# A two-layer encoder step: lead-in on two tiles, products added up in PSUM, and token sums begun a tile sooner

## The chip, the cores and the metric

One core of a Trainium2 chip runs the whole program; the other cores are idle. The metric is the device time of one execution in microseconds, the median of several runs. The engines are named as the profile names them: PE (TensorE), DVE (VectorE), ACT (ScalarE), POOL (GpSimd), SP (the queue that issues most DMAs).

## What is computed

Two layers run over 640 rows (512 of a prompt, 8 x 16 of decode streams) of 1024 features. Every layer is

```
h = rmsnorm(x, g0)
a_x, a_b, a_c, dq, dk, dv, fq, fk, fv, ff, pu = split(h @ w_in)
o = (short_conv, differential_attention, forgetting_attention, pooling)
merged = sum_i sigmoid(h @ w_gate[i] + b_gate[i]) * (o[i] @ w_branch[i])
x = x + rmsnorm(merged @ w_out, g1)
h2 = rmsnorm(x, g2); gu = h2 @ w_ffn_in
x = x + rmsnorm((silu(gu[:, :F]) * gu[:, F:]) @ w_ffn_out, g3)
```

with F = 2816. The keys and values of the new rows are outputs too.

## The kernel before

Activations lie transposed in SBUF: 1024 features as eight blocks of 128 partitions, 640 rows as columns. Every matrix is split into a high and a low half (fp32r), and every product is made as high x high + high x low + low x high. ACT copies the high half of a weight (`whi`, `copy`), DVE subtracts it from the raw one to get the low half (`wlo`, line 274); `w_split` queues these two beforehand, `flush` sends the pending subtractions to DVE.

The order of the instructions on each engine is the order in which the program is written: generators for attention, gates and products are driven in turn by a planner (`drive`), which hands out work by a count of units, and timers (`after`, `tick`) place side work at a number of units. Each engine works through its queue in order, so an instruction whose inputs are not there holds up all behind it on that engine. `s` are tiles from 33 slots (`alloc`, `free`; `NSLOT`) that are handed out in turn; PSUM has the banks S (2), D (2 pairs), O and T (1 each).

**Start** (`first`, lines 1933 to 1955): x comes in five tiles of 128 rows, two halves each. For each tile `norm1` squares the rows on ACT (line 344), takes the root on POOL (338) and scales by root and norm weight on DVE (353); `norm2` transposes on PE (361) into S banks and splits into Ph (ACT) and Pl (DVE, 120). The norm weights come by one DMA per half that spreads a row over 128 partitions. `ab_start` makes the first two input products: the first `CUT` = 384 columns (tiles 0 to 2) of both, then the rest, with the work on the last tiles as hooks among the matmuls. The same `ab_start` with the same `CUT` starts each later pair after a mix (`mix_phase`, `start`): three more times. There tile 3 is turned after 2 of the 8 steps of the first product and tile 4 after 6 of the 8 of the second.

**Gates** (`gates`, `strassen_gates`): the third gate phase is made by a seven-product scheme on halves of the matrix (weights `gs`). It needs sums of the rows' halves, `token_sums`: for each of two parts ten adds of 128x640 on DVE (line 483), then splits into high and low. Timers place them from feature block `GATE_F` = 3 on, one per 0.8 x `GATE_STEP` units, while the last decode units of the attention still run. Four slots per part are taken at the first add. The weights' block sums, `weight_sums`, run on POOL (451). `product` (1532) makes 12 matmuls of 320 columns into one bank.

**Feed-forward** (`strassen`, from line 1841): the same seven products for 19 of 22 column blocks per layer. In both, the products are added up by DVE (`add`, 1844 and 1538) in the tiles s1, u2, u3, c22; product 4 is added to product 0 in s1 and goes to ACT's Silu (1863) or tanh (1541), products 3 and 6 are both added to u2.

Of the kernel before, what the change touches and what calls it, by code (L numbers as in the profile page):

```python
# [23 lines left out]
DFF = 2816  # L24
NJ = DFF // 128
HT = T // 2
CUT = 384
NEG = -1e30
BIG = 3.0e38
NSLOT = 33  # L30
ORDER = [0, 1, 2, 3, "v", 4, 5, 6, 7, 12, 13, 9, 10, 14, 11, 15, 8]
P0N = 7
PACE = [2.2] * 16 + [1.8] * 16 + [1.8] + [3.6] * 8 + [5.05] * 9
# [2 lines left out]
FTS = 0.938  # L36
FT0 = 0.0
J0 = 3
GATE_F = 3
GATE_STEP = 0.8  # L40
FO_ORDER = (4, 0, 1, 2, 3, 5, 6, 7, 8, 9, 10)
EPS = 1e-6

# [17 lines left out]
def encoder_step(ctx: ExitStack, tc: tile.TileContext, I, O):  # L61
# [42 lines left out]
    def psS():  # L104
        return pss.tile([128, 512], F32, tag="S", name=nm("S"))
# [248 lines left out]
            xn.append(s)  # L354
        return xn

    def norm2(xn, hi, lo, t):
        for h in range(2):
            ps = psS()
            for c in range(4):  # L360
                PE.transpose(ps[:, c * 128:(c + 1) * 128], xn[h][:, c * 128:(c + 1) * 128], ident)
            pv = ps.rearrange("p (c n) -> p c n", c=4)
            split(hi[:, 4 * h:4 * h + 4, t * 128:(t + 1) * 128], lo[:, 4 * h:4 * h + 4, t * 128:(t + 1) * 128], pv)
            free(xn[h])
# [24 lines left out]
            if k < 7:  # L389
                yield 0.5  # L390

    def ab_start(keys, x, hooks, evac_fn):
        w = []
        Ds = [psD(), psD()]
        for i in range(2):
            w.append([w_sub(keys[i], p, 0) for p in range(2)])
            if i == 0:
                w_split(sidx[keys[1], 1])
                flush()
            dense(Ds[i], w[i], x, (0,), hooks[i])  # L400
        for i in range(2):
            dense(Ds[i], w[i], x, (1,))
            evac_fn(i, Ds[i])
            if i == 0:
                w_ahead(keys[1], 1)
                flush()

    def v2(t):
        return t.rearrange("p (a b) -> p a b", a=2)
# [3 lines left out]
    def big(tag):  # L413
        return hpool.tile([128, 8, T], F32R, tag=tag, name=nm(tag))

    x_first = [load_x(I["x"], t) for t in range(2)]
    g_first = load_g(0, 0)
    ident = const("ident", C_ID, 128)
    mhalf = cpool.tile([128, 8], F32, tag="mhalf", name="mhalf")
    G.memset(mhalf, -0.5)  # L420
    one1 = cpool.tile([128, 1], F32, tag="one1", name="one1")
# [41 lines left out]
    def token_sums(h, dst, at, step=0.6):  # L463
        hv = [f32(x) for x in h]

        def quad(x, r, c, q):
            return hv[x][:, 4 * r + 2 * q:4 * r + 2 * q + 2, c * HT:(c + 1) * HT]

        t = {}
        P_, M_ = ALU.add, ALU.subtract  # L470
        steps = [(0, (0, 1), (0, 0, 0), M_), (0, None, (1, 0, 1), P_), (0, None, (1, 0, 0), M_),
                 (1, (1, 1), 0, M_), (1, None, (1, 1, 1), P_),
                 (3, 1, (0, 1, 0), M_), (3, None, (1, 1, 0), M_),
                 (2, (1, 1), (0, 0, 1), M_), (2, None, (1, 1, 1), P_), (2, None, (1, 0, 1), M_)]

        def form(n, q):
            if n == 0:
                t[q] = [alloc() for _ in range(4)]
            i, a, b, op = steps[n]
            o = v2(t[q][i])  # L480
            a = o if a is None else v2(t[q][a]) if isinstance(a, int) else quad(0, *a, q)
            b = v2(t[q][b]) if isinstance(b, int) else quad(*b, q)
            V.tensor_tensor(out=o, in0=a, in1=b, op=op)
            if n == len(steps) - 1:
                t["formed"] = q

# [509 lines left out]
    def layer(l, Htag, Otag, hT, first_units):  # L996
# [489 lines left out]
        def prepare_gates(f):  # L1486
            if f == 2:
                load_gates(0)
            elif f == GATE_F:
# [12 lines left out]
                gq["t"] = token_sums(hT, dst, 1.0, GATE_STEP)  # L1502
            elif f == 7:
                gate_sums(0)
                need(lambda: gq["t"].get("formed") == 1)
                for k in range(4):
                    src = v2(gq["t"][k // 2][3])[:, k % 2]
                    split(hi[:, k, HT:], lo[:, k, HT:], src)
                free(*[gq["t"][q][3] for q in range(2)])

        def strassen_gates(br, branch):
# [9 lines left out]

            post = []

            def product(ps, n, p):
                wh, wl = w_sub(("gs", l, n), p)
                while post:
                    post.pop(0)()
                xh, xl = moving[p]
                for k in range(4):
                    a, b = wh[:, k * 128:(k + 1) * 128], wl[:, k * 128:(k + 1) * 128]  # L1530
                    for pi, (w, x) in enumerate(((a, xh), (a, xl), (b, xh))):
                        PE.matmul(ps[:, :HT], w, x[k], start=(k == 0 and pi == 0), stop=(k == 3 and pi == 2))  # L1532
                    if k == 1:
                        yield
                out["p"] = ps[:, :HT]
# [12 lines left out]
            for n in range(4):  # L1548
                f = 2 * n
                ta, tb, X, Y = alloc(), alloc(), alloc(), alloc()  # L1550
                s1, u2, u3, c22 = X[:, :HT], X[:, HT:], Y[:, :HT], Y[:, HT:]
                yield from product(psO(), n, 0)
                copy(s1, out["p"])
                yield
                if pend:
# [8 lines left out]
                if pend:  # L1564
                    branch(f - 1, [pend[1]])
                    yield
                yield from product(psT(), n, 3)
                add(c22, out["p"], u3)
                add(u2, out["p"], u2)
                tanh(tb, 1, c22, f + 1)  # L1570
                gate_sums(n + 1)
                yield
                yield from product(psD()[:, 0, :], n, 4)
                add(s1, out["p"], s1)
                tanh(ta, 0, s1, f)
# [5 lines left out]
                yield from product(psS(), n, 6)  # L1581
# [244 lines left out]
        def product(ps, j, p):  # L1826
            wh, wl = w_sub(("fs", l, j), p)
            xh, xl = moving[p]
            for k in range(4):
                a, b = wh[:, k * 128:(k + 1) * 128], wl[:, k * 128:(k + 1) * 128]  # L1830
                for pi, (w, x) in enumerate(((a, xh), (a, xl), (b, xh))):
                    PE.matmul(ps[:, :HT], w, x[k], start=(k == 0 and pi == 0), stop=(k == 3 and pi == 2))  # L1832
                if k == 1:
                    flush()
                    tick(1.0)
            return ps[:, :HT]

        def strassen(j):
# [4 lines left out]
            def add(out, a, b, op=ALU.add):  # L1843
                V.tensor_tensor(out=out, in0=a, in1=b, op=op)  # L1844

            p1 = product(psO(), j, 0)
            for fn in tail[:1]:
                fn()
            copy(s1, p1)
# [5 lines left out]
            p7 = product(psS(), j, 2)  # L1855
            add(u3, p7, u2)
            sums(j + 1)
            p5 = product(psT(), j, 3)
            add(c22, p5, u3)
            add(u2, p5, u2)  # L1860
            p2 = product(psD()[:, 0, :], j, 4)
            add(s1, p2, s1)
            A.activation(out=act[:, :HT], in_=s1, func=AF.Silu)  # L1863
            p4 = product(psD()[:, 0, :], j, 5)
            if j == NJ - 1:
                convert(0)
            add(s1, u3, p4, ALU.subtract)
            add(act[:, :HT], act[:, :HT], s1, ALU.mult)
            p3 = product(psS(), j, 6)
            add(u2, p3, u2)  # L1870

            def gate():
# [57 lines left out]
    with tc.manual_schedule():  # L1930
        h0 = (big("Ph"), big("Pl"))

        def first(evac_fn):
            xn = {}
            turned = lambda t: norm2(xn.pop(t), h0[0], h0[1], t)
            def normed(t):
                xn[t] = norm1(x_first[t], g_first)
                free(*x_first[t])

            normed(0)  # L1940
            normed(1)
            turned(0)
            normed(2)
            turned(1)
            w_split(1)
            flush(G)
            turned(2)
            normed(3)

            def mid():  # L1950
                normed(4)
                turned(3)

            ab_start([("in", 0, c) for c in ORDER[:2]], h0, ({4: mid}, {6: lambda: turned(4)}), evac_fn)
            free(*g_first)

        layer(0, "P", "Q", h0, first)
# [152 lines left out]
```

## Time and profile before

| | us |
|---|---|
| median of 3 runs | 2091.82 |
| lowest and highest | 2089.9, 2094.06 |
| profiled execution | 2095.22 |
| its span, first instruction to last | 2093.4 |
| PE busy in it | 2038.4 (97%) |
| DVE busy | 1491.2 (71%) |
| ACT busy | 981.7 (47%) |
| POOL busy | 429.6 (21%) |

The granted clock of PE is full in nearly every slice of the page. A busy share says little about a single stretch, so the views that matter are PE's waits (who it waited for, how long in total, how often) and the timeline of each engine around them. In a timeline row the first number is the start, the second the time until the last of the merged instructions ended, and the bracket the idle time of the engine before it with what ended that.

### The profile page before, as it was taken

What the parts mean: (1) busy time and instruction counts of PE and PEld (TensorE: products, weight loads), DVE (VectorE), ACT (ScalarE), POOL (GpSimd) and SP (SyncE); (2) the same over time, 40 slices, a digit from 0 to 9 for tenths busy, and PEclk for the clock granted to TensorE, in tenths of its full rate; (3) what the DMA queues carried; (4) which work ended last, traced back from release to release, by engine and by line L of the source; (5) the groups of instructions that cost most, each with busy time, mean ns of one, the idle gap of its engine ahead of it and who ended that gap; (6) DMA issues with size and microseconds to landing.
All of it is one profiled execution on the core that took longest, in us unless ns stands there. A gap on an engine that the chain in (4) does not pass through costs nothing. (4 is left out here: it accounts for less than half of the span.)

```text
span 2093.4 us, 34625 instructions
## 1 busy us (share of the span) xinstructions
PE 2038.4 (97%) x13050; PEld 1928.6 (92%) x13050; DVE 1491.2 (71%) x2914; ACT 981.7 (47%) x2100; POOL 429.6 (21%) x450
## 2 busy tenths in 40 slices
PE   7999999998999999999999999999999999999998
PEld 7999999998989999988889999999988899999887
DVE  5687478698769889853375774876986698888432
ACT  5656355554444344343256553555544443444431
POOL 3211000113013444400040100001130234443000
PEclk9999999999999999999999999999999999999999
DMA  4312244342341222222523122444313422221223
GB/s 148 109 62 79 81 146 140 119 134 73 102 168 62 91 88 84 81 81 71 171 82 110 68 77 82 151 151 141 111 46 130 153 71 90 88 82 61 101 91 121
DMA packets 100743, 214.35 MB, mean 102 GB/s; under 512 B 10896, under 2 KB 35056, under 8 KB 100576
## 3 DMA queue, kind: packets, MB, share of 16 engines
q1 hardware_dynamic: 99552, 209.16, 29.9%
q0 software_dynamic: 1024, 2.98, 0.4%
q8 instruction: 102, 1.67, 0.3%
q14 instruction: 65, 0.53, 0.1%
HBM read 196.02 MB, written 16.08 MB: 101 GB/s over the span
## 5 line engine op out<-in xcount | busy, mean ns | idle before, releaser
L274 DVE TENSOR_TENSOR wlo<-raw,whi 128x512 fp32r<-128x512 f32 (+2 forms) x388 | 267.5, 694 | 160.0 <-ACT whi L117 155.5
L117 ACT ACTIVATE whi<-raw 128x512 fp32r<-128x512 f32 (+2 forms) x390 | 230.5, 606 | 168.6 <-issue 70.6
L274 DVE TENSOR_TENSOR wlo<-s,whi 128x512 fp32r<-128x512 f32 x196 | 205.3, 1048 | 17.5 <-ACT whi L117 16.1
L117 ACT ACTIVATE s<-s 128x512 fp32r<-128x512 f32 (+7 forms) x294 | 175.0, 619 | 77.6 <-DVE s L1420 45.6
L376 PE MATMUL D<-Ph,whi 128*128 128x320 f32 (+2 forms) x736 | 176.9, 315 | 0.9 <-DVE s L1412 0.9
L376 PE MATMUL D<-Qh,whi 128*128 128x320 f32 (+2 forms) x736 | 176.0, 313 | 0.9 <-DVE s L1412 0.9
L376 PE MATMUL D<-Pl,whi 128*128 128x320 f32 (+2 forms) x736 | 173.6, 310 | 0.0
L376 PE MATMUL D<-Ph,wlo 128*128 128x320 f32 (+2 forms) x736 | 173.6, 310 | 0.0
L376 PE MATMUL D<-Qh,wlo 128*128 128x320 f32 (+2 forms) x736 | 172.8, 309 | 0.0
L376 PE MATMUL D<-Ql,whi 128*128 128x320 f32 (+2 forms) x736 | 172.8, 309 | 0.0
L117 ACT ACTIVATE whi<-s 128x512 fp32r<-128x512 f32 x196 | 117.2, 621 | 42.2 <-PE S L1832 18.9
L338 POOL TENSOR_TENSOR r<-ms,mhalf 128x1 f32<-128x1 f32 x40 | 22.0, 551 | 542.1 <-DVE ms L1672 470.4
L376 PEld LDWEIGHTS D<-Ph,whi 128*128 128x128 f32 x736 | 123.0, 189 | 3.6 <-DVE s L1412 1.4
L376 PEld LDWEIGHTS D<-Pl,whi 128*128 128x128 f32 x736 | 125.2, 189 | 0.6 <-DVE Pl L120 0.4
L376 PEld LDWEIGHTS D<-Qh,whi 128*128 128x128 f32 x736 | 122.5, 188 | 3.4 <-DVE s L1412 1.5
L376 PEld LDWEIGHTS D<-Ql,whi 128*128 128x128 f32 x736 | 124.7, 188 | 0.2
L376 PEld LDWEIGHTS D<-Ph,wlo 128*128 128x128 f32 x736 | 124.8, 189 | 0.0
L376 PEld LDWEIGHTS D<-Qh,wlo 128*128 128x128 f32 x736 | 124.3, 188 | 0.0
L744 POOL CAST s<-s 128x16 fp32r<-128x16 f32 x128 | 30.8, 264 | 407.5 <-DVE s L1420 98.2
L451 POOL TENSOR_TENSOR s<-V,V 128x512 f32<-128x512 f32 x48 | 76.1, 1584 | 172.5 <-DMA V<-in_w_fi 85.3
L117 ACT ACTIVATE s<-T 128x320 fp32r<-128x320 f32 (+6 forms) x132 | 50.9, 386 | 106.5 <-PE T L515 62.5
L1863 ACT ACTIVATE s<-s 128x320 f32<-128x320 f32 x38 | 17.9, 472 | 148.4 <-DVE s L1844 148.4
(480 smaller groups left out, 5890.5 us busy)
## 6 DMA issues: line engine op xcount, KB each, us to landing
raw<-in_w_gate SPq DMA_DIRECT2D x48, 512.0 KB, 3.6
raw<-in_w_fi SPq DMA_DIRECT2D x48, 512.0 KB, 3.5
raw<-in_w_fo SPq DMA_DIRECT2D x44, 512.0 KB, 3.5
V<-in_w_fi SPq DMA_DIRECT2D x80, 256.0 KB, 3.0
raw<-in_w_in SPq DMA_DIRECT2D x32, 512.0 KB, 3.3
s<-in_ck_d SPq DMA_DIRECT2D x32, 256.0 KB, 4.1
s<-in_cv_d SPq DMA_DIRECT2D x32, 256.0 KB, 4.1
s<-in_ck_f SPq DMA_DIRECT2D x32, 256.0 KB, 4.1
```

The lines of the kernel that those rows point to most:

```text
L117: A.activation(out=out, in_=in_, func=AF.Copy, scale=scale)
L274: E.tensor_tensor(out=lo, in0=raw, in1=hi, op=ALU.subtract)
L338: G.tensor_tensor(out=out, in0=ssum, in1=mhalf[:, :n], op=ALU.pow)
L376: PE.matmul(Dt[:, h, :c1 - c0], a, b[:, k, c0:c1], start=(start and pi == 0), stop=(stop and pi == 2))
L451: G.tensor_tensor(out=o[:, :512], in0=x, in1=y, op=op)
L744: G.tensor_copy(out=dst[:, 512:KEYS], in_=f32(src[:, 16 * b:16 * b + 16]))
L1863: A.activation(out=act[:, :HT], in_=s1, func=AF.Silu)
```

## The change

`first` loads each norm-weight row once, as 1 x 512, on ACT's DMA queue, and two matmuls with a row of ones spread them over the partitions in a D bank (`gp`). The first two tiles read them there, and ACT copies them to SBUF for the others. `CUT` becomes 256, everywhere: the first part of the first pair covers tiles 0 and 1; in `first` tile 2 is turned after three of eight steps, tiles 3 and 4 later, and some transposes use banks T and O. The early weight split goes to DVE instead of POOL. In both seven-product schemes product 4 is accumulated onto product 0 in bank O, and product 6 onto product 3 in bank T; the two adds fall away. `token_sums` begin at block 2 with a step of 1.0, take each slot at its first use, and there are 36 slots, for which the scratch of POOL's DMAs is halved.

```diff
-CUT = 384
+CUT = 256
-NSLOT = 33
+NSLOT = 36
-GATE_F = 3
-GATE_STEP = 0.8
+GATE_F = 2
+GATE_STEP = 1.0
...
-    x_first = [load_x(I["x"], t) for t in range(2)]
-    g_first = load_g(0, 0)
+    g_first = [alloc(), alloc()]
+    for h in range(2):
+        A.dma_start(out=g_first[h][:1, :512], in_=gbc[0, 0:1, h * 512:(h + 1) * 512])
+    ones = cpool.tile([1, 128], F32, tag="ones", name="ones")
+    G.memset(ones, 1.0)
+    x_first = [load_x(I["x"], 0)]
     ident = const("ident", C_ID, 128)
+    x_first.append(load_x(I["x"], 1))
+    gp = psD()
+    for h in range(2):
+        PE.matmul(gp[:, h, :], ones, g_first[h][:1, :512], start=True, stop=True)
...
-            if n == 0:
-                t[q] = [alloc() for _ in range(4)]
             i, a, b, op = steps[n]
+            if a is not None:
+                t.setdefault(q, {})[i] = alloc()
...
-            p1 = product(psO(), j, 0)
+            pa, pb = psO(), psT()
+            p1 = product(pa, j, 0)
...
-            p5 = product(psT(), j, 3)
+            p5 = product(pb, j, 3)
             add(c22, p5, u3)
-            add(u2, p5, u2)
-            p2 = product(psD()[:, 0, :], j, 4)
-            add(s1, p2, s1)
-            A.activation(out=act[:, :HT], in_=s1, func=AF.Silu)
+            p2 = product(pa, j, 4, True)
+            A.activation(out=act[:, :HT], in_=p2, func=AF.Silu)
...
-            p3 = product(psS(), j, 6)
+            p3 = product(pb, j, 6, True)
             add(u2, p3, u2)
...
             normed(0)
             normed(1)
+            for h in range(2):
+                copy(g_first[h][:, :512], gp[:, h, :])
             turned(0)
+            w_split(0)
+            flush()
+            turned(1, (psT, psO))
             normed(2)
-            turned(1)
-            w_split(1)
-            flush(G)
-            turned(2)
             normed(3)
...
-    nc = bacc.Bacc("TRN2", target_bir_lowering=False, num_devices=1)
+    nc = bacc.Bacc("TRN2", target_bir_lowering=False, num_devices=1, dynamic_dma_scratch_size=8192)
```

The gates' `strassen_gates` is changed in the same way as `strassen`. In the new file lines from 428 on stand 8 to 11 further down (483 is 493, 1420 is 1430, 1844 is 1853).

Where DVE's queue changes, first while the decode units of the forgetting attention run and the second gate phase is at feature block 3, layer 0. Before, from the split of a branch weight on (`rz`, `z`, `m` and `nm` belong to the softmax of a decode unit):

```order
L274 TENSOR_TENSOR wlo_5440<-raw_5275,whi_5439 128x256
L946 RECIPROCAL rz_5353<-z_5352 64x1
L771 MEMSET s_5458 64x128
L775 TENSOR_SCALAR s_5458<-s_5354,rz_5353 64x512
L775 TENSOR_SCALAR s_5458<-s_5354,rz_5353 64x16
L274 TENSOR_TENSOR wlo_5479<-raw_5399,whi_5478 128x512
L933 ISA s_5534,m_5530<-S_5518,s_5534 64x264
```

And now, from the same split on:

```order
L274 TENSOR_TENSOR wlo_5447<-raw_5282,whi_5446 128x256
L493 TENSOR_TENSOR s_5464<-Ph_139 128x640
L956 RECIPROCAL rz_5360<-z_5359 64x1
L781 MEMSET s_5467 64x128
L785 TENSOR_SCALAR s_5467<-s_5361,rz_5360 64x512
L785 TENSOR_SCALAR s_5467<-s_5361,rz_5360 64x16
L493 TENSOR_TENSOR s_5464<-s_5464,Pl_140 128x640
L274 TENSOR_TENSOR wlo_5489<-raw_5406,whi_5488 128x512
L493 TENSOR_TENSOR s_5464<-s_5464,Pl_140 128x640
L493 TENSOR_TENSOR s_5529<-Ph_139,s_5464 128x640
```

Four token sums (L493) now stand in this block; before, the first of them came one block later. Counted from the merge (L1412, now L1422) of the next block but one to the seven products, 15 sums were left before and 10 are now.

The second place is DVE's queue at the entry of the gate products, layer 0, where the low halves for products 1, 2 and 3 are made. Before:

```order
L274 TENSOR_TENSOR wlo_6193<-s_6177,whi_6192 128x512
L1412 SCALAR_TENSOR_TENSOR s_6137<-s_6137,D_6195 128x640
L1420 TENSOR_TENSOR s_4713<-s_4713,s_6137 128x640
L120 TENSOR_TENSOR s_6159<-s_5948,s_6158 128x640
L274 TENSOR_TENSOR wlo_6226<-s_6178,whi_6225 128x512
L274 TENSOR_TENSOR wlo_6248<-s_6176,whi_6247 128x512
```

Now:

```order
L274 TENSOR_TENSOR wlo_6200<-s_6184,whi_6199 128x512
L1422 SCALAR_TENSOR_TENSOR s_6144<-s_6144,D_6202 128x640
L120 TENSOR_TENSOR s_6148<-s_6058,s_6147 128x640
L274 TENSOR_TENSOR wlo_6233<-s_6185,whi_6232 128x512
L1430 TENSOR_TENSOR s_4720<-s_4720,s_6144 128x640
L274 TENSOR_TENSOR wlo_6256<-s_6183,whi_6255 128x512
```

The merge (L1420, now L1430) has moved from ahead of product 2's low half to behind it, and stands ahead of product 3's.

The third place is DVE's queue in one column block of the feed-forward part, layer 0, from product 3 (bank T) on. Before:

```order
L1844 TENSOR_TENSOR s_9921<-T_9986,s_9921 128x320
L1844 TENSOR_TENSOR s_9920<-T_9986,s_9920 128x320
L274 TENSOR_TENSOR wlo_10011<-s_9831,whi_10010 128x512
L1844 TENSOR_TENSOR s_9920<-D_10009,s_9920 128x320
L274 TENSOR_TENSOR wlo_10030<-V_9847,whi_10029 128x512
L1844 TENSOR_TENSOR s_9920<-s_9921,D_10028 128x320
L1844 TENSOR_TENSOR s_9919<-s_9919,s_9920 128x320
```

Now (another block of the same kind):

```order
L1853 TENSOR_TENSOR s_9426<-T_9428,s_9426 128x320
L274 TENSOR_TENSOR wlo_9518<-s_9345,whi_9517 128x512
L274 TENSOR_TENSOR wlo_9536<-raw_9360,whi_9535 128x512
L1853 TENSOR_TENSOR s_9425<-s_9426,D_9534 128x320
L1853 TENSOR_TENSOR s_9424<-s_9424,s_9425 128x320
```

The second add from T and the add from D, whose sum ACT's Silu read, are gone; the two weight splits follow each other.

## Rows read from the trace of the kernel before

**Rows 1.** Timeline of the lead-in, all engines: start, duration, what, idle before.

```profile
5.45 0.55 POOL L338 TENSOR_TENSOR r<-ms,mhalf 128x1 f32<-128x1 f32 x1 [4.57 <-DVE ms L347]
7.89 0.63 ACT L344 ACTIVATE s<-s 128x512 f32<-128x512 f32 x1 [1.66 <-DMA s<-in_x]
9.73 1.42 DVE L353 SCALAR_TENSOR_TENSOR s<-s,r,s 128x512 f32<-128x512 f32 x2 [4.43 <-DMA s<-in_g_norm]
...
19.32 0.69 PE L376 MATMUL D<-Ph,whi 128*128 128x384 f32 x1
...
31.89 0.28 PE L376 MATMUL D<-Ph,whi 128*128 128x256 f32 x1
```

**Rows 2.** Busy time by stretch at the gate entry: engines' us (instructions), PEclk, DMA.

```profile
490.00:495.00 5.00, 5.00 (x21) 5.00 (x20) 2.93 (x6) 0.63 (x1) 0.00 (x0) 0.50 0.37 128
495.00:500.00 5.00, 5.00 (x36) 5.00 (x35) 3.40 (x7) 2.78 (x6) 0.00 (x0) 1.00 0.08 30
1511.00:1516.00 5.00, 5.00 (x27) 4.95 (x25) 5.00 (x9) 4.08 (x11) 0.00 (x0) 0.66 0.66 205
```

The five engine columns are PE, PEld, DVE, ACT and POOL.

**Rows 3.** Timeline of PE at the gate entries of layer 0 and 1.

```profile
475.92 1.47 PE L803 MATMUL O<-s,s 128*128 128x256 f32 x10 [2.09 <-DVE s L788]
...
488.88 0.63 PE L1532 MATMUL S<-s,wlo 128*128 128x320 f32 x1 [3.51 <-DVE wlo L274]
...
1510.57 1.46 PE L803 MATMUL O<-s,s 128*128 128x256 f32 x10 [2.06 <-DVE s L788]
...
1523.35 0.63 PE L1532 MATMUL S<-s,wlo 128*128 128x320 f32 x1 [2.41 <-DVE wlo L274]
```

**Rows 4.** PE's waits, whole span: us in total, times, longest.

```profile
PE S L1832 <- DVE wlo L274: 4.7, 11, 0.5
PE T L1532 <- DVE wlo L274: 2.6, 4, 0.7
```

**Rows 5.** Timelines of PE and DVE where layer 0's feed-forward part starts, and 256-column matmuls.

```profile
615.80 0.34 PE L376 MATMUL D<-Qh,whi 128*128 128x384 f32 x1
...
624.05 1.04 PE L361 MATMUL S<-ident,s 128*128 128x128 f32 x8
...
621.29 1.42 DVE L353 SCALAR_TENSOR_TENSOR s<-s,r,s 128x512 f32<-128x512 f32 x2 [0.73 <-POOL r L338]
...
32.32 0.28 PE L376 MATMUL D<-Ph,whi 128*128 128x256 f32 x1
32.44 0.28 PE L376 MATMUL D<-Pl,whi 128*128 128x256 f32 x1
```

**Rows 6.** Timeline of PE: two plain fp32 matmuls of 512 columns.

```profile
479.95 1.07 PE L817 MATMUL T<-s,summ 128*64 128x512 f32 x2
```

**Rows 7.** Timelines of DVE and POOL ahead of layer 0's gate products.

```profile
427.52 0.42 DVE L933 CUSTOM_DVE_ANT_0 s<-S,s 64x264 f32<-64x264 f32 x1 [3.49 <-ACT s L117]
...
434.94 0.82 DVE L483 TENSOR_TENSOR s<-Ph 128x640 f32<-128x640 f32 x1
...
483.45 1.90 DVE L1420 TENSOR_TENSOR s<-s,s 128x640 f32<-128x640 f32 x1
485.27 1.88 DVE L120 TENSOR_TENSOR s<-s,s 128x640 fp32r<-128x640 f32 x1
487.07 3.43 DVE L274 TENSOR_TENSOR wlo<-s,whi 128x512 fp32r<-128x512 f32 x2
...
483.38 6.58 POOL L451 TENSOR_TENSOR s<-s,s 128x512 f32<-128x512 f32 x4 [8.60 <-DMA s<-in_w_gate]
```

**Rows 8.** Feed-forward part: one group of DVE, then timelines of ACT, DVE, PE.

```profile
L1844 DVE TENSOR_TENSOR s<-D,s 128x320 f32<-128x320 f32 x38 | 18.3, 481 | 0.7 <-PE D L1832 0.7
...
1754.46 0.47 ACT L1863 ACTIVATE s<-s 128x320 f32<-128x320 f32 x1 [3.91 <-DVE s L1844]
...
1755.49 0.69 DVE L274 TENSOR_TENSOR wlo<-raw,whi 128x512 fp32r<-128x512 f32 x1 [1.06 <-ACT whi L117]
...
1759.44 0.41 PE L1832 MATMUL S<-Qh,wlo 128*128 128x320 f32 x1 [0.40 <-DVE wlo L274]
```

More of the change, by code (lines that the diff above doesn't have):

```diff
@@ L355, in norm1, with norm2 @@
         return xn
-    def norm2(xn, hi, lo, t):
+    def norm2(xn, hi, lo, t, banks=None):
         for h in range(2):
-            ps = psS()
+            ps = banks[h]() if banks else psS()
             for c in range(4):
@@ L390, in dense_steps, with ab_start @@
                 yield 0.5
-    def ab_start(keys, x, hooks, evac_fn):
+    def ab_start(keys, x, hooks, evac_fn, then=None):
         w = []
@@ L400, in ab_start @@
             dense(Ds[i], w[i], x, (0,), hooks[i])
+        if then:
+            then()
         for i in range(2):
@@ L1488, in prepare_gates @@
                 load_gates(0)
-            elif f == GATE_F:
+            if f == GATE_F:
                 gq["t2"] = {}
@@ L1522, in strassen_gates, with product @@
             post = []
-            def product(ps, n, p):
+            def product(ps, n, p, more=False):
                 wh, wl = w_sub(("gs", l, n), p)
@@ L1531, in product @@
                     for pi, (w, x) in enumerate(((a, xh), (a, xl), (b, xh))):
-                        PE.matmul(ps[:, :HT], w, x[k], start=(k == 0 and pi == 0), stop=(k == 3 and pi == 2))
+                        PE.matmul(ps[:, :HT], w, x[k], start=(not more and k == 0 and pi == 0), stop=(k == 3 and pi == 2), skip_group_check=more)
                     if k == 1:
@@ L1551, in strassen_gates @@
                 s1, u2, u3, c22 = X[:, :HT], X[:, HT:], Y[:, :HT], Y[:, HT:]
-                yield from product(psO(), n, 0)
+                pa, pb = psO(), psT()
+                yield from product(pa, n, 0)
                 copy(s1, out["p"])
@@ L1566, in strassen_gates @@
                     yield
-                yield from product(psT(), n, 3)
+                yield from product(pb, n, 3)
                 add(c22, out["p"], u3)
-                add(u2, out["p"], u2)
                 tanh(tb, 1, c22, f + 1)
@@ L1572, in strassen_gates @@
                 yield
-                yield from product(psD()[:, 0, :], n, 4)
-                add(s1, out["p"], s1)
-                tanh(ta, 0, s1, f)
+                yield from product(pa, n, 4, True)
+                tanh(ta, 0, out["p"], f)
                 yield
@@ L1580, in strassen_gates @@
                 yield
-                yield from product(psS(), n, 6)
+                yield from product(pb, n, 6, True)
                 add(u2, out["p"], u2)
@@ L1824, in layer, with product @@
         tail = []
-        def product(ps, j, p):
+        def product(ps, j, p, more=False):
             wh, wl = w_sub(("fs", l, j), p)
@@ L1831, in product @@
                 for pi, (w, x) in enumerate(((a, xh), (a, xl), (b, xh))):
-                    PE.matmul(ps[:, :HT], w, x[k], start=(k == 0 and pi == 0), stop=(k == 3 and pi == 2))
+                    PE.matmul(ps[:, :HT], w, x[k], start=(not more and k == 0 and pi == 0), stop=(k == 3 and pi == 2), skip_group_check=more)
                 if k == 1:
@@ L1844, in add @@
                 V.tensor_tensor(out=out, in0=a, in1=b, op=op)
-            p1 = product(psO(), j, 0)
+            pa, pb = psO(), psT()
+            p1 = product(pa, j, 0)
             for fn in tail[:1]:
@@ L1934, in first @@
             xn = {}
-            turned = lambda t: norm2(xn.pop(t), h0[0], h0[1], t)
+            turned = lambda t, pss_=None: norm2(xn.pop(t), h0[0], h0[1], t, pss_)
             def normed(t):
-                xn[t] = norm1(x_first[t], g_first)
+                xn[t] = norm1(x_first[t], [gp[:, h, :] for h in range(2)] if t < 2 else g_first)
                 free(*x_first[t])
@@ L1951, in mid @@
                 normed(4)
-                turned(3)
-            ab_start([("in", 0, c) for c in ORDER[:2]], h0, ({4: mid}, {6: lambda: turned(4)}), evac_fn)
+                turned(3, (psT, psO))
+            ab_start([("in", 0, c) for c in ORDER[:2]], h0, ({3: lambda: turned(2)}, {4: mid}), evac_fn, lambda: turned(4))
             free(*g_first)
```

## The prediction

> **What bounds the kernel now.** I read the page first, then PE's waits, then the timeline engine by engine in the stretches that the change touches, and last the stretches by engine with the granted clock. By the page PE is busy almost throughout and DVE for some seven tenths of the span (the table above). So only time in which PE waits, or runs at its lower clock, can be won; work taken from DVE counts only where DVE is what PE waits for. There are four such places. In the lead-in the first real product starts at 19.32, and the first vector step waited 4.43 us for the norm weights [rows 1]. At the entry of the gate products PE waits four times, 2 to 3.5 us each, and runs afterwards at half clock [rows 2, 3]. In the feed-forward products it waits for weight splits, 4.7 us in 11 waits, and in the gate products 2.6 us in 4 [rows 4]. Between the mixes and the next products it does not wait; the slack there is small, and the change eats it [rows 5].
>
> **The sum's base.** The rows are from one execution of 2095.22 us (span 2093.4 and 1.8 around it). The median of the runs shown is 2091.82, 0.16% lower; the terms are differences and are taken from the median. About 0.2%, 4.2 us, is what a measurement of this kernel can tell from no change.
>
> **Lead-in.** The 128-row broadcast of the norm weights becomes two rows of 2 KB and two matmuls of one row. The reciprocal root is there at 5.45 + 0.55 = 6.0, the vector step starts at 9.73 [rows 1]: up to 3.7 us come off if the two rows and the two matmuls are done by 6.0. No row shows such a matmul; the nearest, two of 512 columns in the decode units' end, took 1.07 us at full clock [rows 6], so up to 2.1 at half clock. The rows are issued first of all, on ACT's own queue. Bounds: no gain (they come late) and the full 3.7; I take nearly all of it, since the first x half is there by then too. Tile 1 is then next late: its second half is squared at 7.89 [rows 1], the root follows some 1.5 us later, so its vector steps start at about 9.5 at the latest. Laying each tile's rows behind one another (two vector steps 1.42, two splits 1.28, as in the rows of tile 0 and 1), I get first product matmul at 11 to 12 instead of 19.32, with waits between, since three more tiles and four weight splits (two of them taken over from POOL) now stand on DVE's queue; DVE then has about 2.8 us per tile and 0.65 per split, 16.6 us in all from 6.0, so the last tile is ready at 24 to 26. The second halves start there instead of at 31.89 [rows 1], but are 384 columns wide instead of 256: a 256-column matmul follows another after 0.12 us [rows 5], a 384-column one after (624.05 - 615.80 - 0.8) / 42 = 0.177 [rows 5], so 48 of them take 2.7 us longer. I take 31.9 - 25.9 - 2.7 = **-3.3 us**; ends 0 and -5.5.
>
> **The other three starts share the cut.** The start of each later product pair uses the same constant. PE runs 42 matmuls between the start at 615.80 and the last tile's transposes at 624.05; at 256 columns they take 42 x 0.12 = 5.0 us and eight earlier transposes 0.8, so PE arrives at 621.6. The vector step that feeds them runs from 621.29 for 1.42, that is until 622.7 [rows 5], and the work before it does not depend on these matmuls. The first four transposes wait until 622.0, the other four until 622.7: about 0.75 us lost, three times: **+2.2 us** (0 to +4). Here the cover that hid the last tile is cut, and this is a loss.
>
> **Entry of the gate products.** The waits are 2.09 and 3.51 us in layer 0, 2.06 and 2.41 in layer 1 [rows 3], 10.1 us. After them the clock is halved: from 490 to 495 only 21 matmuls start at a granted 0.50, in the next 5 us 36 at 1.00, a loss of 15/36 x 5 = 2.1 us, and the same again in layer 1; after its first wait 27 start instead of 36, 1.25 us [rows 2]. Together 15.5 us. The engine waited for is DVE, whose queue is full there (5.00 of 5 us from 1511 to 1516 [rows 2]). Of the twenty sums of 0.82 us each, the first stands at 434.94, while at 427.52 DVE had just idled 3.49 us [rows 7]. The change puts four of them in that idle time and five fewer behind it (the order shows both): 3.3 to 4.1 us of backlog less. The first wait, for a step that DVE reaches 2 us late, should go: -4.15 and 1.25 of clock. The second is for a weight split behind a merge of 1.90 and a split of 1.88, both about twice 0.82 [rows 7]. In the new order the merge stands behind the weight split, so 1.9 comes off twice: -3.8, and 2.1 us stay. The order also spreads the sums over more matmuls (step 1.0), which keeps their last ones where they were, so I count nothing for that. Of the rest of the clock's loss, 4.2, I take three quarters, as the waits left are under 2 us: -3.2. Sum **-12.4 us**, ends 0 and -15.5. The three slots cost no instruction; they let the sums begin while the attention's buffers are held.
>
> **Two products in PSUM.** 76 adds in the feed-forward part and 16 in the gates go; each is about 0.48 us [rows 8], 44 us of DVE, and most of it saves nothing, since DVE is not late there. But one chain does end at PE. ACT's Silu at 1754.46 had waited 3.91 us for the add of the second product; the next weight's high half stands behind it on ACT, DVE's low half at 1755.49 waited 1.06 us for that, and PE waited 0.40 for the following one [rows 8]. Without the add the Silu reads PSUM when PE is done, at least 0.48 us sooner, and that is over the 0.40 that PE waits. So I count the feed-forward waits as gone, **-5 us** (0 to -7.3, the latter with the gates' 2.6 [rows 4]). The products keep their number of matmuls and start no sooner; banks O and T are held for up to seven products, and the next first writer needs a reader that ended two or three products earlier, so no new wait is counted there.
>
> **Sum.** -3.3 + 2.2 - 12.4 - 5 = -18.5: **2073.3 us**; by the profiled execution 2076.7.
>
> **Rivals.** *POOL still covers the splits.* POOL's block sums for the next product run from 483.38 for 6.58 us, and two weight splits under them took 3.43 [rows 7], 1.7 each. Their data is fetched by a DMA that SP issues behind a DVE split; if DVE is earlier, so are they, and the overlap moves along. Then only the first waits and their 1.25 us go: -5.4 instead of -12.4, **2080.3**. The Trainium skill (SBUF — State Buffer, "Who interferes with whom") has the rule for it: a VectorE instruction with two SBUF inputs contends with GpSimd reads for a shared port pair, one with a single SBUF input does not. By that rule the removed adds, with one input in PSUM, were never the slowed ones, and the sum would be this rival's; the trace agrees on the two-input side, 1.88 against 0.82 us for the same shape [rows 7].
> *All of it goes.* No wait and no slow clock at the gates, and the gates' later waits vanish too: -3.3 + 2.2 - 15.5 - 7.3, **2067.9**.
> *The backlog is not what sets the wait.* The gates and the feed-forward stay as they are: -3.3 + 2.2, **2090.7**. Against it: DVE is busy without a pause between the first wait and the second.
> *The sums hit the attention.* They now start while DVE still serves the decode units, and PE waits for a DVE step of every unit, as it does at 475.92 for 2.09 us [rows 3]. Four units in each layer would cost 8 x 2.1 = 16.6 us, nothing would be won at the gates: 2091.8 - 1.1 - 5 + 16.6 = **2102.3**. It decides if the four sums (3.3 us) no longer fit the idle time before 435; the one gap at 427.52 is 3.49 us, so they fit with little to spare.
>
> **How the numbers follow.** Forecast 2073.3: 0.50. POOL covers: 0.20. All goes: 0.12. Not the backlog: 0.10. Attention: 0.08. The first three are faster by over 0.2%: 0.82; the fourth is within: 0.10; the last slower: 0.08. The range leaves out the last two and reaches from 2063 (the third with a lead-in of -5.5 and a little more at the starts) to 2088 (the second with nothing won in the feed-forward part and the lead-in).
>
> **What would show it.** Right: first 256-column matmul near 12 and the end of the first pair about 3 us sooner; no wait for the attention's low half at the gate entry, the next one under 2 us, and few stretches at 0.50 there; Silu waiting for PE and not for DVE. Three waits of about 0.75 us for the vector step at the starts. Wrong: a gate wait of over 3 us with POOL's sums beside it, or waits for DVE inside the attention between 420 and 470.

## The result, and the profile after

The changed kernel took 2069.57 us (median of 4 runs, 2068.19 to 2071.54), the kernel before beside it 2092.07. The ratio is 0.9893, 95% interval 0.9876 to 0.9911: 22.4 us less (18.6 to 25.9), where 18.5 were forecast. The profiled execution took 2071.54 us, its span is 2069.8.

PE's waits over the whole span (engine, bank and line that waited, what for; total us, times, longest). Those of before that matter are in [rows 3, 4]; these are of the changed kernel:

```profile
PE S L361 <- DVE s L353: 5.9, 6, 2.3
PE O L1279 <- DVE wlo L274: 4.2, 2, 2.1
...
PE T L1542 <- DVE wlo L274: 1.5, 1, 1.5
PE S L1542 <- DVE wlo L274: 1.1, 2, 0.9
PE O L1542 <- DVE wlo L274: 1.1, 1, 1.1
...
PE T L1636 <- DVE s L1853: 0.5, 2, 0.3
```

The waits for the attention's low half (2.09 and 2.06 in [rows 3]) and all those of the feed-forward products are gone. The gate products' wait of 3.51 in layer 0 has become 1.09; that of 2.41 in layer 1 has become two, of 0.94 and 1.47. The last line is new: it is a wait in the products that follow the feed-forward part's column blocks. PE by stretch at the two gate entries, before and then after (engines' us with instructions, granted clock, DMA share, GB/s):

```profile
470.00:500.00 30.00, 24.05 (x138) 21.99 (x137) 26.30 (x35) 15.20 (x37) 9.13 (x6) 0.89 0.24 79
1500.00:1530.00 30.00, 25.53 (x140) 23.48 (x139) 27.80 (x36) 13.02 (x33) 10.84 (x7) 0.83 0.25 84
```

```profile
470.00:500.00 30.00, 28.77 (x188) 26.75 (x188) 25.07 (x39) 16.42 (x41) 12.64 (x8) 1.00 0.26 84
1500.00:1530.00 30.00, 27.43 (x174) 24.98 (x174) 25.27 (x36) 15.07 (x36) 12.13 (x8) 1.00 0.28 96
```

In the same 30 us PE starts 50 and 34 matmuls more, and the granted clock is 1.00 instead of 0.89 and 0.83.

**Where the time went.** For every PE instruction that two traces have in common, its start before less its start in the other is the gain up to there; the growth of that number over a stretch is the stretch's gain. So worked out from the profiled executions (us; lead-in: the gain at 45; gates: 465 to 580 and 1495 to 1615 of before, for e9 from 435 and 1440; later start: layer 1's first projections, 1030 to 1080; feed-forward: 635 to 975 and 1668 to 2005):

| kernel | lead-in | gates | one later start | feed-forward | ratio of runs |
|---|---|---|---|---|---|
| after | 0.9 | 18.4 | -0.84 | 11.0 | 0.9893 |
| e1_psum | 0.6 | 3.3 | 0.00 | 9.2 | 0.9964 |
| e2_sums | 1.6 | 17.6 | -0.02 | -2.9 | 0.9937 |
| e3_lead | 0.5 | 4.2 | -0.83 | 1.4 | 1.0014 |
| e4_cut384 | 1.1 | 18.7 | 0.00 | 9.3 | 0.9878 |
| e6_gcopy | 1.2 | 19.8 | -0.02 | 11.1 | 0.9864 |
| e7_p4 | 0.6 | 2.2 | -0.01 | 9.6 | 0.9955 |
| e8_p6 | 1.1 | 4.1 | 0.05 | 1.6 | 0.9990 |
| e9_step | 0.9 | 17.4 | -0.83 | 10.7 | 0.9889 |
| e10_f3 | 0.6 | 10.0 | -0.84 | 11.3 | 0.9924 |
| e11_slots | 0.4 | 10.6 | 0.05 | -0.1 | 0.9975 |
| e12_turn4 | 2.5 | 18.7 | 0.05 | 9.1 | 0.9863 |
| e13_nosum | 1.6 | 24.2 | -0.85 | 9.2 | 0.9854 |

Such a table must be read with its controls. e3, e7 and e8 change nothing at the gates and yet show 4.2, 2.2 and 4.1 there; the profiled execution of before, 2095.22 against a median of 2092, was a poor one in that place. Its granted clock says why: 0.89 and 0.83 in the two stretches above, while e3 has

```profile
470.00:500.00 30.00, 23.85 (x146) 21.79 (x145) 27.64 (x38) 15.28 (x38) 9.50 (x6) 0.94 0.26 84
1500.00:1530.00 30.00, 26.36 (x163) 24.08 (x162) 29.69 (x39) 14.90 (x37) 10.84 (x7) 0.94 0.26 84
```

That is an estimated 30 x (0.11 + 0.17) = 8.4 us lost to the clock at most (a slow clock costs nothing while PE waits) against 3.6, with nothing changed there. The mean over the four kernels with unchanged gates (0 for before) is 2.6; I take it off below, and as these four range from 0 to 4.2, a difference of 2 us at the gates is no finding. In the feed-forward part the kernels that leave it unchanged range from -2.9 to 1.4. The lead-in's control is its spread: unchanged it ends 0 (before), 0.6, 1.6, 0.6, 1.1 and 0.4 earlier, by how soon its first transfers land.

### The profile page after: what moved, and what is told of

Read it like the earlier page. It is cut to its first block, busy times and chain, and to the rows that moved or that the text cites. A ratio compares the mean times of both kernels' runs of the same rounds, so it can differ in the third digit from the quotient of the medians.

```text
span 2069.8 us, 34511 instructions
## 1 busy us (share of the span) xinstructions
PE 2034.4 (98%) x13054; PEld 1925.4 (93%) x13054; DVE 1455.2 (70%) x2824; ACT 987.2 (48%) x2102; POOL 426.2 (21%) x449
## 4 chain that ended last, share of the span: by engine, by line
PE 86%; DVE 6%; issue 2%; ACT 2%; DMA 2%; POOL 2%; SPq 0%; DVEq 0%; POOLq 0%; ACTq 0%
PE D L376 26%; PE D L1636 11%; PE O L1841 6%; PE S L1841 6%; PE T L1841 6%; PE D L1418 5%; PE T L1636 3%; PE O L1636 3%; PE D L1841 3%; PE O L813 2%; PE D L1279 2%; PE T L1542 1%; PE O L1542 1%; DVE wlo L274 1%; PE S L1542 1%
## 5 line engine op out<-in xcount | busy, mean ns | idle before, releaser
L274 DVE TENSOR_TENSOR wlo<-s,whi 128x512 fp32r<-128x512 f32 x196 | 198.8, 1015 | 26.9 <-ACT whi L117 25.8
L117 ACT ACTIVATE whi<-s 128x512 fp32r<-128x512 f32 x196 | 121.5, 626 | 49.0 <-PE S L1841 36.1
L754 POOL CAST s<-s 128x16 fp32r<-128x16 f32 x128 | 36.4, 308 | 395.1 <-PE O L813 159.0
L461 POOL TENSOR_TENSOR s<-V,V 128x512 f32<-128x512 f32 x48 | 71.9, 1497 | 154.6 <-DMA V<-in_w_fi 79.2
L117 ACT ACTIVATE s<-O 32x64 f32<-32x64 f32 (+1 forms) x174 | 47.6, 274 | 95.7 <-PE O L813 67.7
```

Source lines behind the costliest of these rows:

```text
L117: A.activation(out=out, in_=in_, func=AF.Copy, scale=scale)
L274: E.tensor_tensor(out=lo, in0=raw, in1=hi, op=ALU.subtract)
L461: G.tensor_tensor(out=o[:, :512], in0=x, in1=y, op=op)
L754: G.tensor_copy(out=dst[:, 512:KEYS], in_=f32(src[:, 16 * b:16 * b + 16]))
```

## The experiments

**e1_psum**: the accumulation alone.

```diff
-            p2 = product(psD()[:, 0, :], j, 4)
-            add(s1, p2, s1)
-            A.activation(out=act[:, :HT], in_=s1, func=AF.Silu)
+            p2 = product(pa, j, 4, True)
+            A.activation(out=act[:, :HT], in_=p2, func=AF.Silu)
...
-            add(u2, p5, u2)
...
-            p3 = product(psS(), j, 6)
+            p3 = product(pb, j, 6, True)
...
```

> The kernel before with the accumulation in PSUM alone (feed-forward part and gates). By the offsets of PE's instructions between the two traces the feed-forward part gave 6.1 us in layer 0 and 4.9 in layer 1, and the two gate entries 10.4 and 8.5. Theory (the parts are independent, PSUM gives the feed-forward gain and what the gates lose after their entry, 3.0 us per layer in the stretch behind it): 2092 - 11 - 6 = 2075. Rival 1 (the adds matter only where the feed-forward part waits): 2092 - 11 = 2081. Rival 2 (the lighter DVE queue, not the sums' place, empties the whole gate entry too): 2092 - 11 - 19 = 2062.

2082.5, ratio 0.9964 (0.9950 to 0.9977). The feed-forward part gives 9.2 us; at the gates 3.3 is 0.7 above the control. Rival 1 holds: PSUM works in the feed-forward part, and at the gates it shows no gain that is clear of the control.

**e2_sums**: the sums' place, step and slots alone.

```diff
-NSLOT = 33
+NSLOT = 36
-GATE_F = 3
-GATE_STEP = 0.8
+GATE_F = 2
+GATE_STEP = 1.0
...
-            if n == 0:
-                t[q] = [alloc() for _ in range(4)]
             i, a, b, op = steps[n]
+            if a is not None:
+                t.setdefault(q, {})[i] = alloc()
...
```

> The kernel before with the token sums' new place and step, the slots taken at first use, 36 slots and the halved scratch. Theory: the two waits per entry and the clock behind them go, 2092 - 13 = 2079, the feed-forward part unchanged; PE's waits for the attention's low half at the entry are gone. Rival 1 (the wait only changes its place): within 2 us of 2092. Rival 2 (it gives all of the 19 us at the gates alone): 2073.

2076.97, ratio 0.9937 (0.9923 to 0.9951): 13 us. The gates give 17.6, 15 beyond the control; PE's waits for the attention's low half are gone. The feed-forward part loses 2.9: its waits grow from 4.7 to 8.2 us with no change of its code. In layer 1 the weight splits whose input POOL made take 1182 ns in the middle instead of 1053. That POOL's sums now lie over DVE's splits in another way would fit this, but it was not shown.

**e3_lead**: the lead-in and the cut alone (with the scratch halved, to fit).

```diff
-CUT = 384
+CUT = 256
...
+    gp = psD()
+    for h in range(2):
+        PE.matmul(gp[:, h, :], ones, g_first[h][:1, :512], start=True, stop=True)
...
```

> The kernel before with the lead-in and the cut at 256 columns in all four starts. The offsets of the two traces give -0.9 us up to the first projection and +0.8 to 1.2 at each of the three later starts. Theory: 2092 - 0.9 + 2.9 = 2094, slower by 0.1%. Rival (the starts' loss came from the other parts of the change, the lead-in from its own): 2091.

2093.08, ratio 1.0014 (1.0006 to 1.0023): slower, as expected.

**e4_cut384**: the changed kernel, with 256 columns in the first start alone.

```diff
 CUT = 256
+CUT2 = 384
...
-                ab_start(nx, (nxt["hi"], nxt["lo"]), ({2: mid}, {6: lambda: turned(4)}), evac_fn)
+                ab_start(nx, (nxt["hi"], nxt["lo"]), ({2: mid}, {6: lambda: turned(4)}), evac_fn, None, CUT2)
...
```

> The changed kernel with 256 columns in the first start alone and 384 again in the three later ones. Theory (the cut hid the last tile's norm there): the waits of the later starts go, 2069.6 - 2.9 = 2066.7. Rival 1 (what the starts lose is given back by a later wait for DVE): within 1 us of 2069.6. Rival 2 (the loss comes from the lead-in's other bank order or from the earlier gates): no change at the starts, 2069.6.

2064.4, ratio 0.9878 (0.9862 to 0.9895), against 0.9893 of the change; this difference is inside the intervals, the traces decide. The one later start that no change of clock touches loses 0.83 to 0.85 us in every kernel with 256 columns and nothing in any with 384. The other two later starts show it too, less cleanly: 0.9 to 1.1 and 0.8 to 1.1 with 256 columns, 0.15 to 0.24 and 0 to 0.24 with 384 (600 to 635 and 1640 to 1668 of before). The turns of the last two tiles in layer 0's feed-forward start, changed kernel and then e4 (in e4 these lines stand one further down):

```profile
606.72 1.25 PE L361 MATMUL S<-ident,s 128*128 128x128 f32 x8
...
612.41 1.29 PE L361 MATMUL S<-ident,s 128*128 128x128 f32 x8 [0.19 <-DVE s L353]
```

```profile
604.80 1.04 PE L362 MATMUL S<-ident,s 128*128 128x128 f32 x8
...
612.00 1.04 PE L362 MATMUL S<-ident,s 128*128 128x128 f32 x8
```

**e6_gcopy**: e4, with ACT's copies of the norm weights behind the first tile's turn.

```diff
+            turned(0)
             for h in range(2):
                 copy(g_first[h][:, :512], gp[:, h, :])
-            turned(0)
```

> e4_cut384 with ACT's two copies of the spread norm weights moved behind the first tile's turn, so that ACT takes that tile's high halves first. In the changed kernel ACT stands 2.41 us idle ahead of these copies, which start at 10.92, and the first tile's high half starts only at 11.89, though its transposes end at 9.71. Theory (ACT's order is what made the lead-in late): first product matmul near 12 instead of 14.0, end of the first pair 1.5 to 2 us sooner than in e4_cut384, 2064.4 - 1.7 = 2062.7. Rival (the x tiles' arrival or the last tile's norm sets the end): first matmul sooner, end of the first pair unchanged, 2064.4.

2062.76, ratio 0.9864 (0.9849 to 0.9878). The median is the theory's number, but by chance: its interval overlaps e4's, and in the trace the rival holds. ACT took the first tile at 8.79 and not at 11.89 as in the changed kernel, and the first product matmul came at 13.26, not at 14.0, but the second halves start at 27.38, where e4 had 27.55:

```profile
26.09 1.03 PE L362 MATMUL S<-ident,s 128*128 128x128 f32 x8
27.38 0.44 PE L377 MATMUL D<-Ph,whi 128*128 128x384 f32 x1 [0.25 <-ACT Ph L118]
28.11 0.44 PE L377 MATMUL D<-Pl,whi 128*128 128x384 f32 x1 [0.29 <-DVE Pl L121]
```

**e12_turn4**: e6, with the last tile turned two steps earlier.

```diff
-            ab_start([("in", 0, c) for c in ORDER[:2]], h0, ({3: lambda: turned(2)}, {4: mid}), evac_fn, lambda: turned(4))
+            ab_start([("in", 0, c) for c in ORDER[:2]], h0, ({3: lambda: turned(2)}, {4: mid, 6: lambda: turned(4)}), evac_fn)
```

> e6_gcopy with the last tile of the lead-in turned two steps ahead of the end of the second first half instead of behind it. In e6_gcopy its norm is ready at 24.86 and PE turns it at 26.09, the second halves then wait 0.25 for its high half and 0.29 for its low half. Theory: these two waits and their restarts go, end of the first pair 0.8 us sooner than in e6_gcopy, 2062.8 - 0.8 = 2062. Rival (PE reaches the turn before the norm is ready): no change.

The turn moves ahead. Its high half is there when PE comes to need it; its low half is not quite, for the second matmul starts 0.42 us behind the first, where 0.17 to 0.18 is usual:

```profile
24.84 1.04 PE L362 MATMUL S<-ident,s 128*128 128x128 f32 x8
...
26.43 0.34 PE L377 MATMUL D<-Ph,whi 128*128 128x384 f32 x1
26.85 0.45 PE L377 MATMUL D<-Pl,whi 128*128 128x384 f32 x1
```

1.25 us sooner in the trace; the median is 2063.74, ratio 0.9863 (0.9846 to 0.9879), the same as e6 within the measurement. These two are the fastest of the kernels that leave nothing out.

**e7_p4 and e8_p6**: of the two accumulations in the feed-forward part one each, the rest as before.

```diff
-            p2 = product(psD()[:, 0, :], j, 4)
-            add(s1, p2, s1)
-            A.activation(out=act[:, :HT], in_=s1, func=AF.Silu)
+            p2 = product(pa, j, 4, True)
+            A.activation(out=act[:, :HT], in_=p2, func=AF.Silu)
...
```

> The kernel before, in the feed-forward part alone product 4 accumulated onto product 0 (the add in front of Silu goes), product 6 still added by DVE. With both accumulations the feed-forward part gave 5.3 + 3.8 = 9.2 us in e1_psum. Theory of the prediction (the chain add, Silu, high half, low half is what PE waits for): nearly all of it, -8, 0.9962 of before. Rival (DVE's load as such, 38 adds as good as the other 38): half, -4.6, 0.9978 of before.

```diff
-            add(u2, p5, u2)
...
-            p3 = product(psS(), j, 6)
+            p3 = product(pb, j, 6, True)
...
```

> The counterpart of e7_p4: product 6 accumulated onto product 3 (the second add from bank T goes), product 4 still added by DVE in front of Silu. Theory of the prediction: 0 to -1.5 us, 0.9995 of before. Rival (DVE's load): -4.6, 0.9978.

e7: 2081.56, ratio 0.9955 (0.9940 to 0.9969), 9.6 us in the feed-forward part. e8: 2090.24, ratio 0.9990 (0.9980 to 1.0001), 1.6 us, which is no more than e3's 1.4 with that part unchanged. Both take the same 38 adds off DVE, so most of the gain is not due to DVE's load but to the chain through Silu. Not all of e8's small number tells of the load, though. Its seven products themselves give 3.8 us (e7's 9.6), and 2.2 are lost behind them: the first of the products that follow needs bank T, which DVE's add of the last block still holds. In layer 0 of e8 this is

```profile
895.23 0.50 PE L1627 MATMUL T<-whi,s 128*128 128x512 f32 x1 [0.82 <-DVE s L1844]
```

In e8 PE still waits in the seven products,

```profile
PE S L1832 <- DVE wlo L274: 2.8, 7, 0.6
...
PE D L1832 <- DVE wlo L274: 1.0, 3, 0.4
```

and in e7 one wait of 0.2 is left of them. In e7 and in the changed kernel ACT's Silu waits for PE's bank O, as forecast:

```profile
L1871 ACT ACTIVATE s<-O x38: 437/438/438, 659.9 to 1906.7; 128x320 f32<-128x320 f32 x38
its engine sat idle before it (us, times) until:
  PE O L1841: 114.4, 38
```

This is the changed kernel; the figures are the shortest, middle and longest duration in ns, first and last start, and then the idle time ahead in all 38.

**e10_f3**: the changed kernel with the sums' old place and step.

```diff
-GATE_F = 2
-GATE_STEP = 1.0
+GATE_F = 3
+GATE_STEP = 0.8
```

> The changed kernel with the token sums begun at block 3 with step 0.8 as before, all else (slots, accumulation, lead-in) as changed. Theory (the place of the sums frees the entry): both waits for the attention's low half and the long one of over 2.4 us come back, and 14 to 16 us with them: 2081 to 2083 where the changed kernel has 2069.6. Rival (the slots taken at first use, or the accumulation, free it): below 2073.

2075.36, ratio 0.9924 (0.9909 to 0.9939). Neither the theory's time nor the rival's came: the two waits for the attention's low half come back at 1.0 us each, and the long ones at 2.5 and 2.7. The sums' place is worth 18.4 - 10.0 = 8.4 us at the gates (6.5 by the runs), not 14 to 16. The rest stayed, and needed another cause.

**e11_slots**: the kernel before with the slots alone (36, taken at first use, scratch halved).

> The kernel before with 36 slots, the slots of the token sums taken at first use and the halved scratch; the sums stand at block 3 with step 0.8 as before. e10_f3 gave 9.7 us at the gates with the old place of the sums, e1_psum 3.0 without the slots. Theory (the slots let POOL's block sums start sooner, off the splits that PE waits for): 1.7 us per layer in the stretch behind the gates' entry and 1 to 2.5 at the entries, 5 to 7 us in all, 0.997 of before. Rival (slots only hold buffers, and e10_f3's gain needs the accumulation): within 1.5 us of before.

2086.37, ratio 0.9975 (0.9964 to 0.9987), 5.2 us; at the gates 10.6, 8 beyond the control. The halved scratch is not the cause, for e3 has it too; the three slots more and their being taken at first use were not told apart. POOL's first two groups of block sums (line 451) and the first sum of a later one, before and then e11:

```profile
462.41 1.94 POOL L451 TENSOR_TENSOR s<-V,V 128x512 f32<-128x512 f32 x1 [15.78 <-PE O L803]
464.43 2.23 POOL L451 TENSOR_TENSOR s<-s,V 128x512 f32<-128x512 f32 x1
469.62 1.41 POOL L451 TENSOR_TENSOR s<-V,V 128x512 f32<-128x512 f32 x1 [2.96 <-DVE s L1420]
473.18 1.59 POOL L451 TENSOR_TENSOR s<-V,s 128x512 f32<-128x512 f32 x1 [2.15 <-DVE s L753]
...
505.50 1.82 POOL L451 TENSOR_TENSOR s<-V,V 128x512 f32<-128x512 f32 x1 [15.54 <-DVE wlo L274]
```

```profile
464.02 1.63 POOL L451 TENSOR_TENSOR s<-V,V 128x512 f32<-128x512 f32 x1 [19.36 <-PE O L803]
465.72 2.23 POOL L451 TENSOR_TENSOR s<-s,V 128x512 f32<-128x512 f32 x1
467.91 1.85 POOL L451 TENSOR_TENSOR s<-V,V 128x512 f32<-128x512 f32 x1
469.73 1.75 POOL L451 TENSOR_TENSOR s<-V,s 128x512 f32<-128x512 f32 x1
...
499.74 1.29 POOL L451 TENSOR_TENSOR s<-V,V 128x512 f32<-128x512 f32 x1 [8.71 <-ACT s L1541]
```

Before, POOL stood still 2.96 and 2.15 us in the middle of a group, for DVE to end with a tile; with three more it works through, and the later group starts 5.8 us sooner. Then the sums no longer lie over this part of DVE's work. Two token sums at the entry, before and then in e11:

```profile
469.79 1.92 DVE L483 TENSOR_TENSOR s<-s,Pl 128x640 f32<-128x640 f32 x1
...
473.58 1.89 DVE L483 TENSOR_TENSOR s<-s,Pl 128x640 f32<-128x640 f32 x1
```

```profile
472.41 0.81 DVE L483 TENSOR_TENSOR s<-s,Pl 128x640 f32<-128x640 f32 x1
...
475.09 0.81 DVE L483 TENSOR_TENSOR s<-s,Pl 128x640 f32<-128x640 f32 x1
```

PE's waits for the attention's low half fall from 4.2 to 2.0 us, and the four waits of bank T (2.6 us, [rows 4]) are gone. They lay behind the entries (498 to 580 and 1532 to 1615 of before), and there the control is tight, -0.2 to 0.0: e11 gains 3.4 there, e10 and the changed kernel 4.3, e1 1.0.

**e13_nosum**: the changed kernel without POOL's block sums in the gates.

```diff
-            G.tensor_tensor(out=o[:, :512], in0=x, in1=y, op=op)
+            if key[0] == "gs":
+                G.memset(o[:, :512], 0.0)
+            else:
+                G.tensor_tensor(out=o[:, :512], in0=x, in1=y, op=op)
```

> The changed kernel with POOL's block sums of the gate weights replaced by POOL writing zeros into their tiles, so four of the seven gate products take wrong weights; the feed-forward part keeps its sums. Theory (what is left of the gates' waits is POOL's sums lying over DVE's splits): the splits at the entry take 0.68 instead of up to 1.8 us, the waits of 1.1, 0.9 and 1.5 us go, 2069.6 - 4.5 = 2065. Rival (it is DVE's queue or ACT's high halves): waits unchanged, 2069.

2061.75, ratio 0.9854 (0.9840 to 0.9869): 8 us less than the change. No wait of the gate products is left, and the gates give 24.2. In the changed kernel DVE's splits at layer 1's entry lie under POOL's sums, POOL's row and then DVE's:

```profile
1502.81 6.61 POOL L461 TENSOR_TENSOR s<-s,s 128x512 f32<-128x512 f32 x4 [10.67 <-DMA s<-in_w_gate]
```

```profile
1504.71 1.76 DVE L274 TENSOR_TENSOR wlo<-s,whi 128x512 fp32r<-128x512 f32 x1
1506.39 1.91 DVE L1430 TENSOR_TENSOR s<-s,s 128x640 f32<-128x640 f32 x1
1508.22 1.75 DVE L274 TENSOR_TENSOR wlo<-s,whi 128x512 fp32r<-128x512 f32 x1
```

DVE pauses nowhere between these rows, so PE's waits there (0.94 and 1.47) are not for sums that came late: DVE itself is slower. At the same place of e13 the splits take 0.68 and the merge 0.82:

```profile
1496.29 0.68 DVE L274 TENSOR_TENSOR wlo<-s,whi 128x512 fp32r<-128x512 f32 x1
1496.89 0.82 DVE L1433 TENSOR_TENSOR s<-s,s 128x640 f32<-128x640 f32 x1
1497.63 0.68 DVE L274 TENSOR_TENSOR wlo<-s,whi 128x512 fp32r<-128x512 f32 x1
```

The zeros that POOL writes in e13 slow nothing down: they run from 1490.49 for 1.93 us, and the merge at 1491.73 takes 0.82.

**e9_step**: the changed kernel with `GATE_STEP = 0.8`.

> The changed kernel with the token sums' step back at 0.8, their start at block 2 kept. The prediction counted nothing for the step. Theory: gate entries within 1 us of the changed kernel's (7.9 + 2.0 and 6.2 + 2.0 us of gain against before). Rival (denser sums stand in front of DVE's steps for the decode units): 2 to 4 us of it lost, new waits of PE for DVE between 430 and 475.

2069.66, ratio 0.9889 (0.9872 to 0.9906): no difference. Both theories held in part. At 1.2 us each the two waits for the attention's low half are back, which costs 1.5 us per layer ahead of the entry; the entries themselves then give 20.4 instead of 18.4 (the 17.4 of the table counts the loss in). The prediction's nothing for the step was right.

## Why the prediction was right, step by step

**Entry of the gate products** (-12.4 forecast): 18.4 in the trace, 15.8 beyond the control, just past the end of -15.5. Of the 18.4, 14.1 lie at the entries themselves (to 498 and 1532), some 11 beyond the control, near the forecast; 4.3 lie behind them, where the waits of bank T went, which the forecast left out and gave at most to the accumulation. The first waits went and the clock stayed full, as forecast. The second wait, put at 2.1 us, is 1.09 in layer 0 and still 2.41, in two pieces, in layer 1: there the merge, moved behind one split, takes its 1.91 us ahead of the next, so the 1.9 that its new place was to save came off in layer 0 alone. What gained in layer 1 is the first wait and the clock behind both, 1.00 throughout where before had 0.66 from 1511 to 1516 [rows 2]. The step that failed is the cause: the backlog of sums carried all of it, and of the slots the text said that they let the sums begin and cost nothing. Alone, the slots give 8 us by the traces and the place of the sums another 8 (5.2 and 6.5 by the runs). The trace of before had the sign of it: POOL's idle times of 2.96 and 2.15 us within a group of its sums, which I had not read.

**POOL still covers the splits** (the rival at 2080.3): its mechanism is real, and its price was wrong. The overlap did move along (the rows of layer 1 above), and e13 shows that it still costs the changed kernel about 6 us at the gates. But the clock no longer fell behind the second wait, layer 0's second wait shrank, and the feed-forward part gave twice what forecast and rival both counted; in layer 1 its picture, a second wait as long as before, was right. Of the page cited there, the Trainium skill (SBUF — State Buffer, "Who interferes with whom"), both halves now have rows: in the changed kernel, under POOL's sums from 481.17 to 488.71, an add with one input in PSUM keeps its 0.48 us between two splits of 1.77 and 1.37:

```profile
485.79 1.77 DVE L274 TENSOR_TENSOR wlo<-V,whi 128x512 fp32r<-128x512 f32 x1
487.49 0.48 DVE L1548 TENSOR_TENSOR s<-S,s 128x320 f32<-128x320 f32 x1
487.89 1.37 DVE L274 TENSOR_TENSOR wlo<-V,whi 128x512 fp32r<-128x512 f32 x1
```

It is not always DVE that loses. When the first of these sums began at 481.17, DVE's merge at 481.65 and its split at 482.38 kept 0.82 and 0.68, and the sum took 3.04 us instead of 1.29.

**Two products in PSUM** (-5 forecast, at most -7.3): 9 to 11 us in all kernels that have it, past the end of -7.3 too. The chain was right, and e7 against e8 shows it. The size was off by a factor of two: I added up the waits, 5.7 us. A wait of 0.40 at 1759.44 [rows 8] puts that matmul 0.71 us behind the one before it, where 0.147 is usual: it costs 0.56. And short delays are in no list of waits. Over the two feed-forward stretches the matmuls of the seven products that start over 0.2 us behind the one before them were late by 13.6 us in 53 places before, and by 1.4 in 12 after. Of that difference, 12.2, the table shows 11.0, because 1.0 is lost again: the prediction counted no new wait for the banks, but the first product behind the last column block finds T still held (the last line of the waits above, 0.3 us at most, which puts that matmul and the next 0.5 us late in each layer).

**Lead-in** (-3.3 forecast): 0.9 us, the mean of the six traces with the change as it is, and 0.7 in the six with the old lead-in (before with 0 among them), which end up to 1.6 earlier by chance: 0.2 us, next to nothing, inside the range of 0 to -5.5 but not where I put it. The first matmul came at 14.03 and not at 11 to 12. One reason is that ACT's copies of the norm weights stand in front of the first tile's high half, which I had not put on ACT's queue:

```profile
10.92 1.08 ACT L117 ACTIVATE s<-D 128x512 f32<-128x512 f32 x2 [2.41 <-issue]
11.89 1.09 ACT L117 ACTIVATE Ph<-S 128x512 fp32r<-128x512 f32 x2
```

With the copies behind that tile (e6) the first matmul came at 13.26 where e4 has 13.98, so they explain 0.7 us of the 2 to 3, and the end of the pair hardly moved. What set the end was the last tile: turned behind all first halves, its low half was there at 28.4 and not at 25.9. e12 turns it earlier and gets 1.25 us.

**The three starts** (+2.2 forecast): 0.84 in the one that can be read without the clock, and about as much in the other two (e4), so 2.5 for three. Right in mechanism and size; e4 takes it back.

**The sum.** With controls taken off: -0.2 + 2.5 - 15.8 - 10.5 (10.1 on average, and 0.4 that the unchanged parts lose) = -24.0, and -22.4 by the runs, whose interval (18.6 to 25.9) holds both. Part of the difference is a wait of PE in layer 1:

```profile
1343.79 0.56 PE L376 MATMUL D<-Qh,whi 128*128 128x320 f32 x2 [2.06 <-DVE s L1422]
```

It was 0.66 us before. Behind it stands a cache tile that lands too late for ACT. This loss of 0.9 to 1.4 us shows in seven of the eight kernels with the new lead-in (not in e12) and in none of the five others; why the lead-in should reach so far was not settled. That the forecast came near the result is in part luck: the lead-in was put 3 us too high and the feed-forward part 5 too low, and the 4.3 behind the gates' entries were not in it. These errors cancel in part; the runs end 3.9 below the forecast.

## What to carry to other kernels

Where one engine's order is the bound, a lost wait is read from the distances of its instructions, not from the list of waits alone. Before a gain is put down to the work that was moved, look at what the buffers allow other engines to do: three more tiles, taken at first use, let POOL run ahead, and that was about half the gain at the gates. A constant that is shared by several places is priced at each of them: 384 columns were worth 2.5 us in three of four.

## What the runs showed of the hardware

The granted clock falls after like waits in one execution and not in the next. Twice in a row PE waits 1.1 and 2.1 us in the first projections (line 1269, now 1279). Before, and then after:

```profile
59.00:63.00 4.00, 3.88 (x32) 3.89 (x33) 3.91 (x7) 0.88 (x2) 2.07 (x2) 1.00 0.42 132
```

```profile
59.00:63.00 4.00, 4.00 (x23) 4.00 (x23) 3.93 (x7) 1.77 (x3) 1.16 (x1) 0.57 0.39 132
```

The lower of the two levels (1.2 GHz) costs 1.5 us there. It shows in eight of the thirteen kernels other than before, with and without each part of the change, so one profile can't tell whether a wait of that size costs its clock or not; the controls above are the remedy.
